# An output stage's quarters, casts and finishing steps spread out, V's casts moved, and two attention slivers joined

## The chip, the cores and the metric

The kernel runs on one core of a Trainium2 chip. The time is device microseconds from launch to end; before the change the median of three runs is 2045.68 us (2044.66 to 2046.22). The core has an engine for matrix products (PE), a vector engine (DVE), a scalar engine (ACT), a small general one (POOL) and a queue that issues the transfers (SP). Each works through its own instructions in order, and a semaphore holds an instruction back until what it reads is there.

## The reference

One inference step of a hybrid decoder layer: 1024 prompt tokens with 16 learned ones ahead of them, and 8 × 4 sample tokens. The input is normalised and multiplied by one large projection. Half of the width goes to eight heads of stick-breaking attention, half to gated linear attention; both are gated and go through one output projection, then a norm and the residual.

```python
def stick_break_weights(z, mask):
    sp = jnp.where(mask, jax.nn.softplus(z), 0.0)
    later = lax.cumsum(sp, axis=z.ndim - 1, reverse=True) - sp
    return jnp.where(mask, jnp.exp(jax.nn.log_sigmoid(z) - later), 0.0)

def sb_attend(qb, qpos, k, v, kpos, bias):
    a = stick_break_weights(sb_logits(qb, k, bias), kpos[None, :] < qpos[:, None])
    return jnp.einsum('bhqk,bkhd->bqhd', a.astype(v.dtype), v)
...
    mixed = jnp.concatenate([o_sb * jax.nn.silu(sg), o_gla * jax.nn.silu(gg)], axis=-1)
    return mixed @ w_out
```

The sum `later` runs over the keys behind a key, so a block of keys needs the sum of all later blocks first. The result y is x plus the norm of `mixed @ w_out`.

## The kernel before

Every product is made of three matmuls: both operands are split into a high part (a cast to a shorter float, on ACT) and a low part (the difference, on DVE), and hi·hi, hi·lo and lo·hi are added up in PSUM, the memory of 8 banks that PE writes. So each weight tile that arrives (`wr`) costs an ACT cast and a DVE subtraction before PE can use it.

**The order of work.** The stages of the program run one after another: norm and transposes; eight heads; low rank and gates; gated linear attention; the paged values of the samples, with the gate groups; the output stage. Inside a stage a small scheduler of generators, the Weaver `W`, interleaves side work with the products: after a group of products `W.beat()` runs the generators that are due, and `yield n` in a generator means "go on n beats later". A generator only writes instructions down; a list scheduler then orders them on each engine. `spread(ins)` ties an instruction behind the latest marked product `W.mark`, and the manual dependencies called "behind" tie it behind another instruction. Both tie only the order in which the scheduler places instructions; neither makes an engine wait.

**The heads** (L541 to L760). While the input projection of head h runs, the attention of head h−1 is woven in. `attend_tile` makes one tile: keys of block j (126 new keys each) against queries of half qi. It makes z (L609 to L611), a softplus X on ACT (L615 to L619) and DVE (L620), masks on POOL (L623, L639), takes the carry of the block behind (L629), splits X (`hi_s`, `lo_s`, L590 and L593), adds the sums with a triangular matrix (L632, L633), makes Y by an exponential (L637), splits it (`hi_a`, `lo_a`) and multiplies by V into the bank O (L647 to L649). The tiles of a half go from the last block to the first; the half qi = 1 begins with (1,8), 32 queries wide, and qi = 0 with (0,4), 24 wide. The other tiles have 150 to 512 queries. `load_v` (L570 to L585) loads three pieces of V (`vr`), casts them (L582) and takes the low part (L584).

**The output stage** (L1325 to L1690). The projection is made by seven products p of halves of the matrices, in Strassen's manner: pairs (1,2), (6), (5,3) and (7,4), each for q = 0 and 1. A step (p, q) has eight k, and each k takes a weight tile (`ring`, cast at L1429, low part at L1430) and twelve matmuls of 128x512 (L1631 to L1633), four banks by three. `W.beat()` follows each k. Left operands are the forms `f`: quarters of the mixed matrix, loaded from `md` by `quarter` (L1333), added or subtracted (`s3` at L1343, `s2` at L1348, `combined`), and cast (L1375, L1378). `take` empties banks at the end of a step (`u` copies at L1478, sums at L1496 and L1500). `finish0` (L1540 to L1577) finishes the first half of the rows: it loads x (`xr`, L1554), forms y = y · r + x on DVE (L1565) and stores it; afterwards it loads the residual of the second half (L1557). `load_keep` loads and casts eight weight tiles for the last step, and `finish_samples` finishes the sample rows. Each DMA of the queue waits for the eighth before it, and the rings of raw tiles (four of tag `fr`, seven of tag `wr`) are passed on in order.

Of the kernel before, what the change touches and what calls it, by code (L numbers as in the profile page):

```python
# [20 lines left out]
P = 128  # L21
# [19 lines left out]
KT = 126  # L41
# [48 lines left out]
def hybrid_step(ctx: ExitStack, tc: tile.TileContext, x_prompt, x_sample, cache_k, cache_v, state_gla,  # L90
# [447 lines left out]
    with tc.tile_pool(name="sp", bufs=1) as sp, tc.tile_pool(name="sps", bufs=1, space=PSUM) as sps:  # L538
# [5 lines left out]
        cap = sp.tile([P, 1], F32, name="cap")  # L544
        pool.memset(cap[:], 16.0)
        room = sp.tile([P, HEADS], F32, name="room")
        vec.tensor_scalar(room[:], bias0[:], -1.0, 16.0, ALU.mult, ALU.add)
# [22 lines left out]
        def load_v(h, V, behind):  # L570

            for c in range(3):
# [6 lines left out]
                if c == 2:  # L579
                    nc.sync.dma_start(sv[1:33, 2, :], src[8 * KT:REAL])  # L580
                vs = slice(3 * c, 3 * c + 3)
                ins = act.copy(V[0][:, vs, :], sv)  # L582
                tc.add_manual_dep(ins.ins, behind.name, NOSYNC, reason="behind")
                vec.tensor_tensor(V[1][:, vs, :], sv, V[0][:, vs, :].bitcast(F32), ALU.subtract)  # L584
# [13 lines left out]
        def attend_tile(h, qi, qlo, qhi, j, jmax, q, kt, V, carry, O):  # L598
            nm = f"{h}_{qi}_{j}"
            k0 = j * KT  # L600
            nk = P
            c0 = max(qlo, k0)
            col = c0 - qlo
            n = qhi - c0
            qs = slice(c0 - META, c0 - META + n)
            ks = slice(j * P, j * P + nk)
            z = sps.tile([P, 512], F32, tag="z", bufs=4, name=f"z{nm}")
            zz = z[:nk, :n]
            mm(zz, kt[0][:, ks], q[0][:, qs], start=True, stop=False)  # L609
            mm(zz, kt[0][:, ks], q[1][:, qs], start=False, stop=False)  # L610
            mm(zz, kt[1][:, ks], q[0][:, qs], start=False, stop=True)  # L611
# [6 lines left out]
            act.activation(X, X, AF.Exp, scale=-1.0, bias=cap[:nk])  # L618
# [3 lines left out]
            if w > 0:  # L622
                pool.affine_select(X[:, :w], X[:, :w], [[1, w]], ALU.is_gt, 0.0, base=c0 - k0 + 1, channel_multiplier=-1)  # L623
            yield 2
            if j < jmax:
# [8 lines left out]
            carry[qi] = (j, zz, col)  # L634
# [3 lines left out]
            if w > 0:  # L638
                pool.affine_select(Y[:, :w], Y[:, :w], [[1, w]], ALU.is_gt, 0.0, base=c0 - k0 + 1, channel_multiplier=-1)  # L639
# [10 lines left out]
            if j == 0:  # L650
                st = sp.tile([P, 512], F32, tag="X", bufs=3, name=f"ost{h}_{qi}")
                act.copy(st[:], o[:])
                nc.sync.dma_start(od[h][:, qlo - META:qhi - META], st[:])

        def attend(h, q, kt, V):

            carry, O = {}, {}
            for qi, j in ORDER:
                qlo, qhi = ((16, 528), (528, REAL))[qi]
                n = qhi - max(qlo, j * KT)  # L660
                W.spawn(attend_tile(h, qi, qlo, qhi, j, (qhi - 1) // KT, q, kt, V, carry, O))
# [3 lines left out]
        ORDER = [(1, j) for j in range(8, -1, -1)] + [(0, j) for j in range(4, -1, -1)]  # L665
# [6 lines left out]
        def sample_q(h, qsm, ks):  # L672
# [8 lines left out]
            zns = sp.tile([NSMP, NSMP], F32, tag="zns", name=f"zns{h}")  # L681
            act.copy(zns[:], ps[:NSMP, :NSMP])
            nc.sync.dma_start(znd[:, h, :], zns[:])
# [3 lines left out]
        def head(h):  # L687
# [21 lines left out]
            def split_k(raw, c, lo, hi):  # L709
# [10 lines left out]
                if c == 2:  # L720
                    act.copy(ks[:], raw[:, REAL - lo:hi - lo])
# [603 lines left out]
    with ExitStack() as out:  # L1325
# [26 lines left out]
        for k in range(6):  # L1352
            W.spawn(later(k), 26 + 2 * k)
# [29 lines left out]
        def combined(p, k):  # L1383
# [3 lines left out]
            t = quarter(raw(f"q{p}_{k}")[:], p == 4, p in (2, 3, 4), k)  # L1387
# [5 lines left out]

        def form(p, gap):
            if p == 3:
# [334 lines left out]
```

## Time and profile before

| what | value |
|---|---|
| median of the runs | 2045.68 us (2044.66 to 2046.22) |
| the profiled execution, its own time | 2047.26 us |
| its span, first to last instruction | 2045.6 us |
| mean granted PE clock | 0.998 |
| DVE line L470 (scores against paged keys) | 595.0 us, 2048 of 291 ns |
| longest wait of PE, at start-up (L233) | 8.1 us |
| DMA over the span | 301.85 MB, 148 GB/s |

A timeline row gives start, duration, engine, line, operation, written tile <- read tiles, and shape; "x2" joins neighbours of one kind. In square brackets stands how long the engine was idle ahead of it, and which instruction or DMA released it. Where a row says `[0.92 <-DVE lo_s L593]`, PE did nothing for 0.92 us until DVE had written `lo_s`. Matmuls overlap, so the price of one is read from the distance of starts, not from durations. Queries by window give each engine's busy time, the granted clock, the share of the 16 DMA engines and GB/s.

### The profile page before, as it was taken

The numbers are of one execution on the slowest core, as the hardware profiler recorded it, in microseconds if no ns is written. First come the engines' busy times: TensorE is split into PE (matmuls) and PEld (weight loads), VectorE is DVE, ScalarE is ACT, GpSimd is POOL, SyncE is SP. The second block draws the span as 40 slices with busy tenths as digits, with TensorE's granted clock in tenths as the row PEclk, the third lists the DMA queues.
The fourth block names the chain that finished last, engine by engine and source line by source line (L and its number), as shares of the span: only waits on it lengthen the run. The fifth ranks groups of instructions, "written<-read, shape, count | busy, mean of one in ns | idle before, by whom it ended". The sixth has DMA issues, their size and how long they took to land.

```text
span 2045.6 us, 41995 instructions
## 1 busy us (share of the span) xinstructions
PE 2012.9 (98%) x12443; PEld 1859.9 (91%) x12443; DVE 1499.0 (73%) x6171; ACT 1025.6 (50%) x2409; POOL 93.9 (5%) x339
## 2 busy tenths in 40 slices
PE   6999999999999999999999999999999999999998
PEld 5999999999999999999999999999988898788776
DVE  7368888888888888899898888978444347554576
ACT  7366767675766758433535345254334335432332
POOL 0011110101000000100000000000000000000000
PEclk9999999999999999999999999999999999999999
DMA  6355454544555442533343424336767666352475
GB/s 203 101 142 159 131 163 135 163 136 152 154 154 145 144 128 77 141 103 88 104 107 81 130 78 121 89 90 189 237 217 237 223 216 191 130 169 76 145 257 196
DMA packets 371822, 301.85 MB, mean 148 GB/s; under 512 B 42360, under 2 KB 312104, under 8 KB 371592
## 3 DMA queue, kind: packets, MB, share of 16 engines
q1 hardware_dynamic: 371288, 298.64, 48.7%
q8 instruction: 98, 1.61, 0.3%
q14 instruction: 132, 1.08, 0.2%
q10 hardware_dynamic: 304, 0.53, 0.1%
HBM read 241.75 MB, written 57.31 MB: 146 GB/s over the span
## 4 chain that ended last, share of the span: by engine, by line
PE 89%; DMA 4%; DVE 4%; ACT 2%; issue 1%; SPq 1%; DVEq 0%; ACTq 0%
PE acc_g L347 5%; PE acc_g L348 5%; PE acc_g L349 5%; PE b L1631 4%; PE b L1633 4%; PE b L1632 4%; PE acc_gv L347 3%; PE acc_gv L348 3%; PE acc_gv L349 3%; PE acc_k L347 3%; PE acc_k L349 3%; PE acc_k L348 3%; PE acc_q L347 3%; PE acc_q L348 3%; PE acc_q L349 3%; PE acc_v L347 3%
## 5 line engine op out<-in xcount | busy, mean ns | idle before, releaser
L470 DVE SCALAR_TENSOR_TENSOR jk<-kp,qb 128x128 f32<-128x128 f32 x2048 | 595.0, 291 | 44.8 <-DMA qb<-qsd 1.7
L347 PE MATMUL acc_g<-hT,wh_g 128*128 128x368 f32 (+2 forms) x768 | 251.0, 327 | 1.0 <-ACT gx L532 1.0
L348 PE MATMUL acc_g<-hT,wh_g 128*128 128x368 f32 (+2 forms) x768 | 247.2, 322 | 0.0
L349 PE MATMUL acc_g<-hT,wl_g 128*128 128x368 f32 (+2 forms) x768 | 246.9, 322 | 0.0
L470 DVE DVE_READ_ACCUMULATOR jk<-kp,qb 128x1 f32 x2048 | 169.4, 83 | 0.0
L1631 PE MATMUL b<-ring,f 128*128 128x512 f32 x416 | 164.8, 396 | 2.5 <-DVE u L1500 1.1
L1632 PE MATMUL b<-ring,f 128*128 128x512 f32 x416 | 163.2, 392 | 1.0 <-DVE ring L1430 1.0
L1633 PE MATMUL b<-ring,f 128*128 128x512 f32 x416 | 162.5, 391 | 0.0
L347 PEld LDWEIGHTS acc_g<-hT,wh_g 128*128 128x128 f32 x768 | 144.3, 188 | 13.3 <-issue 10.7
L1430 DVE TENSOR_TENSOR ring<-wr,ring 128x512 fp32r<-128x512 f32 x104 | 71.2, 690 | 106.0 <-ACT ring L1429 103.9
L348 PEld LDWEIGHTS acc_g<-hT,wh_g 128*128 128x128 f32 x768 | 144.5, 188 | 0.7
L349 PEld LDWEIGHTS acc_g<-hT,wl_g 128*128 128x128 f32 x768 | 144.2, 188 | 0.0
L1429 ACT CAST ring<-wr 128x512 fp32r<-128x512 f32 x104 | 64.2, 621 | 144.4 <-PE b L1633 89.9
L347 PE MATMUL acc_gv<-hT,wh_gv 128*128 128x402 f32 (+2 forms) x384 | 130.1, 339 | 0.0
L347 PE MATMUL acc_k<-hT,wh_k 128*128 128x384 f32 (+1 forms) x384 | 126.1, 328 | 0.0
L348 PE MATMUL acc_gv<-hT,wh_gv 128*128 128x402 f32 (+2 forms) x384 | 125.3, 326 | 0.0
L349 PE MATMUL acc_gv<-hT,wl_gv 128*128 128x402 f32 (+2 forms) x384 | 125.0, 326 | 0.0
L347 PE MATMUL acc_q<-hT,wh_q 128*128 128x368 f32 (+2 forms) x384 | 125.0, 325 | 0.0
L349 PE MATMUL acc_k<-hT,wl_k 128*128 128x384 f32 (+1 forms) x384 | 124.7, 325 | 0.0
L348 PE MATMUL acc_k<-hT,wh_k 128*128 128x384 f32 (+1 forms) x384 | 124.6, 325 | 0.0
L348 PE MATMUL acc_q<-hT,wh_q 128*128 128x368 f32 (+2 forms) x384 | 123.6, 322 | 0.0
L349 PE MATMUL acc_q<-hT,wl_q 128*128 128x368 f32 (+2 forms) x384 | 123.3, 321 | 0.0
(468 smaller groups left out, 5292.7 us busy)
## 6 DMA issues: line engine op xcount, KB each, us to landing
kp<-in_cache_k_dram SPq DMA_DIRECT2D x512, 64.0 KB, 2.0
vr<-in_cache_v_dram SPq DMA_DIRECT2D x64, 512.0 KB, 5.1
qb<-qsd SPq DMA_DIRECT2D x64, 256.0 KB, 5.6
wr_g<-in_w_in_dram SPq DMA_DIRECT2D x64, 256.0 KB, 3.5
wr<-td SPq DMA_DIRECT2D x56, 256.0 KB, 2.8
tf<-in_w_out_dram SPq DMA_DIRECT2D x48, 256.0 KB, 4.9
td<-tf SPq DMA_DIRECT2D x48, 256.0 KB, 2.5
wr<-in_w_out_dram SPq DMA_DIRECT2D x48, 256.0 KB, 3.5
```

What stands on the lines that cost most here:

```text
L347: mm(acc[c][:, :n], wh, hh[k][:, lo:hi], start=(k == 0), stop=False)
L348: mm(acc[c][:, :n], wh, hl[k][:, lo:hi], start=False, stop=False)
L349: W.mark = mm(acc[c][:, :n], wl, hh[k][:, lo:hi], start=False, stop=(k == NK - 1)).ins
L470: ins = vec.scalar_tensor_tensor(jk[:], kp[:], 1.0, qbs[h, b][:, t, :], ALU.mult, ALU.mult, accum_out=zt[:, t, NPG - 1 - i:NPG - i])
L1429: act.copy(wh, r)
L1430: vec.tensor_tensor(wl, r, wh.bitcast(F32), ALU.subtract)
L1631: mm(bk[:], ah, wh, start=first and k == 0, stop=False, skip_group_check=True)
L1632: mm(bk[:], ah, wl, start=False, stop=False, skip_group_check=True)
L1633: mm(bk[:], al, wh, start=False, stop=last and k == 7, skip_group_check=True)
```

## The change

The diff has three parts.

**One tile for two slivers.** The tiles (1,8) and (0,4) become one tile (`both`) with 64 queries: columns 480 to 511 of both halves of q. Its keys are block 8's, with the 24 keys of block 4 that (0,4) used copied by POOL to rows 32 to 55 of the block; V's rows get the same by a small load, and the masks on POOL cut off what is not to be seen. The carry of half 0 is copied by ACT (`kept`), the product goes to the O bank, is copied by ACT (`ob`), and each half of it is added to the last 32 columns of that half's output on DVE.

```diff
-        def attend_tile(h, qi, qlo, qhi, j, jmax, q, kt, V, carry, O):
+        def attend_tile(h, qi, qlo, qhi, j, q, kt, V, carry, O):
...
-            n = qhi - c0
+            n = 64 if both else qhi - c0
...
+            def queries(t):
+                if both:
+                    return t[:].rearrange("p (a x) -> p a x", a=2)[:, :, 480:512]
+                return t[:, qs]
+
+            def causal(t):
+                if both:
+                    t = t.rearrange("p (a x) -> p a x", a=2)
+                    pool.affine_select(t, t, [[1 - 24, 2], [1, 32]], ALU.is_gt, 0.0, base=24, channel_multiplier=-1)
+                    pool.memset(t[0:32, 0, :], 0.0)
...
+            if both:
+                kept = sp.tile([P, NSMP], F32, tag="ks", name=f"cy{h}")
+                act.copy(kept[0:1, :], z[0:1, 0:32])
+                carry[0], carry[1] = (4, kept, 480), (8, z[:, 32:64], 480)
+            else:
+                carry[qi] = (j, zz, col)
...
+            if both:
+                o = sps.tile([P, 512], F32, tag="O", name=f"Ob{h}")[:, :n]
+                mm(o, V[0][:, j, :], ah[:, :n], start=True, stop=False, skip_group_check=True)
+                mm(o, V[0][:, j, :], al[:, :n], start=False, stop=False, skip_group_check=True)
+                mm(o, V[1][:, j, :], ah[:, :n], start=False, stop=True, skip_group_check=True)
+                O[2] = sp.tile([P, 64], F32, tag="ob", name=f"ob{h}")
+                act.copy(O[2][:], o)
+                return
...
+                vec.tensor_tensor(st[:, 480:512], st[:, 480:512], O[2][:, 32 * qi:32 * qi + 32], ALU.add)
...
-        ORDER = [(1, j) for j in range(8, -1, -1)] + [(0, j) for j in range(4, -1, -1)]
+        ORDER = [(1, j) for j in range(8, -1, -1)] + [(0, j) for j in range(3, -1, -1)]
...
+                    for t in kt:
+                        pool.tensor_copy(t[:, 8 * P + 32:8 * P + 56], t[:, 4 * P + 1:4 * P + 25].bitcast(F32))
```

On PE, in head 0's attention beside the products for k of head 1 (`acc_k1`), before had the three z matmuls of the tile (0,4), of 24 columns (`z0_0_4` is z of head 0, half 0, block 4):

```order
L348 MATMUL acc_k1_0_1897<-hT11_156,wh_k1_2_2202 128x384
L349 MATMUL acc_k1_0_1897<-hT11_156,wl_k1_2_2203 128x384
L609 MATMUL z0_0_4_2277<-q0_0_1077,k0_0_846 128x24
L610 MATMUL z0_0_4_2277<-q1_0_1078,k0_0_846 128x24
L611 MATMUL z0_0_4_2277<-q0_0_1077,k1_0_847 128x24
L347 MATMUL acc_k1_1_1898<-hT10_155,wh_k1_2_2202 128x384
L348 MATMUL acc_k1_1_1898<-hT10_155,wh_k1_2_2202 128x384
```

At the same rows after has the z of the tile (0,3), 150 columns wide:

```order
L348 MATMUL acc_k1_0_1905<-hT11_156,wh_k1_2_2210 128x384
L349 MATMUL acc_k1_0_1905<-hT11_156,wl_k1_2_2211 128x384
L630 MATMUL z0_0_3_2285<-q0_0_1077,k0_0_844 128x150
L631 MATMUL z0_0_3_2285<-q1_0_1078,k0_0_844 128x150
L632 MATMUL z0_0_3_2285<-q0_0_1077,k1_0_845 128x150
L347 MATMUL acc_k1_1_1906<-hT10_155,wh_k1_2_2210 128x384
L348 MATMUL acc_k1_1_1906<-hT10_155,wh_k1_2_2210 128x384
```

The three rows of 24 columns are gone, and (0,3) has moved up into their place; the joined tile stands where (1,8) stood, beside the products for v of head 1, with 64 columns instead of 32:

```order
L349 MATMUL acc_v1_1_1307<-hT1_146,wl_v1_0_1312 128x384
L630 MATMUL z0_1_8_1339<-q0_0_1077,k0_0_844 128x64
L631 MATMUL z0_1_8_1339<-q1_0_1078,k0_0_844 128x64
L632 MATMUL z0_1_8_1339<-q0_0_1077,k1_0_845 128x64
L347 MATMUL acc_v1_2_1308<-hT0_145,wh_v1_0_1311 128x304
```

What moved: 24-column rows are gone, and the half 0 starts with (0,3). In all PE has 11262 rows before and 11198 after.

**V's casts.** `load_v` issues all three loads first, the last piece ahead, and casts them some beats later, each tied to a product.

```diff
-            for c in range(3):
+            rows = []
+            for c in (2, 1, 0):
...
+                rows.append((vs, sv))
+                yield 1
+            yield 1
+            for vs, sv in rows:
                 ins = act.copy(V[0][:, vs, :], sv)
                 tc.add_manual_dep(ins.ins, behind.name, NOSYNC, reason="behind")
+                spread(ins)
```

On ACT, in head 4, the last V cast of before (L582) stands ahead of the whole X chain of the tile (1,7) (`X4_1_7`, L615 to L619):

```order
L682 COPY zns4_8416<-zn4_8414 32x32
L582 CAST V0_4_8310<-vr4_2_8397 128x384
L615 ACTIVATE X4_1_7_8427<-z4_1_7_8423,room_837 128x158
L618 ACTIVATE X4_1_7_8427<-X4_1_7_8427,cap_835 128x158
L619 ACTIVATE X4_1_7_8427<-X4_1_7_8427 128x158
L187 CAST wh_v5_2_8617<-wr_v5_2_8615 128x512
L637 ACTIVATE Y4_1_8_8478<-z4_1_8_8362,bias0_827 128x32
L629 ACTIVATE X4_1_7_8427<-z4_1_8_8362 1x32
L590 CAST hi_s4_1_7_8502<-X4_1_7_8427 128x158
```

In after two casts (L587) stand among that chain and the third behind it:

```order
L636 ACTIVATE X4_1_7_8367<-z4_1_7_8363,gpre_78 128x158
L639 ACTIVATE X4_1_7_8367<-X4_1_7_8367,gpre_78 128x158
L587 CAST V0_4_8254<-vr4_2_8271 128x384
L640 ACTIVATE X4_1_7_8367<-X4_1_7_8367 128x158
L587 CAST V0_4_8254<-vr4_1_8301 128x384
L187 CAST wh_v5_2_8566<-wr_v5_2_8564 128x512
L587 CAST V0_4_8254<-vr4_0_8340 128x384
L657 COPY cy4_8422<-z4_1_8_8304 1x32
L663 ACTIVATE Y4_1_8_8424<-z4_1_8_8304,bias0_827 128x64
L650 ACTIVATE X4_1_7_8367<-z4_1_8_8304 1x32
L596 CAST hi_s4_1_7_8449<-X4_1_7_8367 128x158
```

The X operations now come first; behind the third cast are the carry copy `cy4`, the Y of the joined tile and the carry and `hi_s` of (1,7).

**The output stage.** `early` loads a11 and s3 16 beats apart, `later` starts four beats later, `form` fetches its quarters two ahead and pins the casts of p = 2 from k = 4 on behind the newest `u` copy; quarter loads are tied to products, whose last matmul is now `W.mark` (so `spread` works in this stage). `finish0` takes 1 or 2 beats by turns, ties its DVE operation to a product, and loads the second half's first residuals between its items; `finish_samples` begins three beats later.

```diff
         def quarter(dst, r, c, k):
-            nc.sync.dma_start(dst, md[8 * c + k][:, 512 * r:512 * r + 512])
+            spread(nc.sync.dma_start(dst, md[8 * c + k][:, 512 * r:512 * r + 512]))
...
             quarter(a11[k], 0, 0, k)
+            yield 16
             quarter(s3[k], 1, 0, k)
-            yield 5
+            yield 9
...
-            W.spawn(later(k), 26 + 2 * k)
+            W.spawn(later(k), 30 + 2 * k)
...
-            t = quarter(raw(f"q{p}_{k}")[:], p == 4, p in (2, 3, 4), k)
+            t = quarters.pop((p, k))
...
+            def fetch(k):
+                if k < 8 and p not in (1, 6, 7):
+                    quarters[p, k] = quarter(raw(f"q{p}_{k}")[:], p == 4, p in (2, 3, 4), k)
+
+            if p not in (1, 6, 7):
+                fetch(0)
+                fetch(1)
+                yield 2
...
+                    fetch(k + 2)
+                    while p == 2 and k == 4 and not newest_u:
+                        yield 1
+                    split(f[:, 0], f[:, 1], combined(p, k), (newest_u if k > 3 else evacs)[-1] if p == 2 else None)
...
-                yield 2 if n < 8 else 1
+                yield 2 - n % 2
                 o = sums_[i, b]
-                vec.scalar_tensor_tensor(o, o, r[:, i:i + 1], xs.pop(n), ALU.mult, ALU.add)
+                spread(vec.scalar_tensor_tensor(o, o, r[:, i:i + 1], xs.pop(n), ALU.mult, ALU.add))
...
+                elif n > 7:
+                    i, b = divmod(n - 8, 2)
+                    xr[i, b] = late_[b][:, i * 512:(i + 1) * 512].bitcast(F32)
+                    load_xr(i, b)
...
         def finish_samples():
-            yield 2
+            yield 5
...
-            mm(bk[:], al, wh, start=False, stop=last and k == 7, skip_group_check=True)
+            W.mark = mm(bk[:], al, wh, start=False, stop=last and k == 7, skip_group_check=True).ins
```

On DVE, at the end of step (4,0) and the start of step (7,1), before has ring splits (L1430; `wr71_0` is the weight tile of p = 7, q = 1, k = 0), casts' low parts of `keep` (L1673), the finishing operations of `finish0` (L1565, with `xr1_2` the x of row block 1, column block 2) and the sums `u0` that empty the banks (L1500):

```order
L1673 TENSOR_TENSOR keep3_30995<-keep3_30995 128x512
L1430 TENSOR_TENSOR ring1_29199<-wr40_7_31304,ring0_29198 128x512
L1565 SCALAR_TENSOR_TENSOR y12_0_1_30594<-y12_0_1_30594,vrt_y0_30976,xr1_2_31299 128x512
L1673 TENSOR_TENSOR keep3_30995<-keep3_30995 128x512
L1430 TENSOR_TENSOR ring1_29199<-wr71_3_31408,ring0_29198 128x512
L1565 SCALAR_TENSOR_TENSOR y12_1_1_30937<-y12_1_1_30937,vrt_y0_30976,xr1_3_31362 128x512
L1430 TENSOR_TENSOR ring1_29199<-wr71_0_31342,ring0_29198 128x512
L1565 SCALAR_TENSOR_TENSOR y12_0_2_30599<-y12_0_2_30599,vrt_y0_30976,xr2_2_31384 128x512
L1565 SCALAR_TENSOR_TENSOR y12_1_2_30942<-y12_1_2_30942,vrt_y0_30976,xr2_3_31406 128x512
L1500 TENSOR_TENSOR u0_0_29405<-b70_0_30952,u0_0_29405 128x512
L1500 TENSOR_TENSOR u0_1_29407<-b70_1_30953,u0_1_29407 128x512
L1500 TENSOR_TENSOR u0_2_29409<-b70_2_30954,u0_2_29409 128x512
```

In after the same stretch reads (ring splits at L1481, finishing at L1616, sums at L1551, `keep` at L1724):

```order
L1724 TENSOR_TENSOR keep3_30879<-keep3_30879 128x512
L1616 SCALAR_TENSOR_TENSOR c11_0_29119<-c11_0_29119,vrt_y0_30857,xr3_0_30983 128x512
L1481 TENSOR_TENSOR ring1_29084<-wr40_7_31201,ring0_29083 128x512
L1616 SCALAR_TENSOR_TENSOR c11_1_29120<-c11_1_29120,vrt_y0_30857,xr3_1_31004 128x512
L1481 TENSOR_TENSOR ring1_29084<-wr71_3_31306,ring0_29083 128x512
L1724 TENSOR_TENSOR keep3_30879<-keep3_30879 128x512
L1481 TENSOR_TENSOR ring1_29084<-wr71_0_31244,ring0_29083 128x512
L1616 SCALAR_TENSOR_TENSOR y12_0_0_30475<-y12_0_0_30475,vrt_y0_30857,xr0_2_31075 128x512
L1481 TENSOR_TENSOR ring1_29084<-wr71_1_31262,ring0_29083 128x512
L1551 TENSOR_TENSOR u0_0_29289<-b70_0_30833,u0_0_29289 128x512
L1551 TENSOR_TENSOR u0_1_29291<-b70_1_30834,u0_1_29291 128x512
L1551 TENSOR_TENSOR u0_2_29293<-b70_2_30835,u0_2_29293 128x512
```

Before has three finishing operations between the split of `wr71_3` and the sums `u0_0`, two of them next to each other; after has one there, and those ahead of it belong to the first two column blocks (`c11`), each with a ring split or a `keep` part behind it.

More of the change, by code (lines that the diff above doesn't have):

```diff
@@ L543, in hybrid_step @@
         pool.affine_select(bias0[:], bias0[:], [[0, HEADS]], ALU.is_gt, -1e30, base=P - 1, channel_multiplier=-1)
[L544 to L547, printed above, removed]
+        cap, room = gpre[:, 0:1], gpre[:, HEADS:]
+        pool.memset(cap, 16.0)
+        vec.tensor_scalar(room, bias0[:], -1.0, 16.0, ALU.mult, ALU.add)
         def tok_out(raw, c, lo, hi, h, outp, outs_, nm):
@@ L637, in attend_tile @@
             act.activation(Y, zz, AF.Exp, bias=bias)
[L638 to L639 removed]
+            causal(Y)
             if w > 0:
@@ L680, in sample_q @@
             mm(ps[:NSMP, :NSMP], ks[:], qsm[:], start=True, stop=True)
-            zns = sp.tile([NSMP, NSMP], F32, tag="zns", name=f"zns{h}")
-            act.copy(zns[:], ps[:NSMP, :NSMP])
-            nc.sync.dma_start(znd[:, h, :], zns[:])
+            zns = stage(f"zns{h}")[:NSMP, :NSMP]
+            act.copy(zns, ps[:NSMP, :NSMP])
+            nc.sync.dma_start(znd[:, h, :], zns)
             yield 4
@@ L1439, in hybrid_step @@
             W.spawn(later(k))
-        W.spawn(form(2, 1), 2)
+        W.spawn(form(2, 1), 1)
         W.spawn(form(6, 2), 10)
@@ L1477, in take @@
                 with urgent():
-                    act.copy(u, bk[:])
+                    newest_u.append(act.copy(u, bk[:]).ins)
             elif p == 2:
```

38 lines of the change are left out of this document (19 added, 19 removed).

## The prediction

> **What bounds the kernel now.** The page comes first.
>
> ```profile
> span 2045.6 us, 41995 instructions
> ...
> PE 2012.9 (98%) x12443; PEld 1859.9 (91%) x12443; DVE 1499.0 (73%) x6171; ACT 1025.6 (50%) x2409; POOL 93.9 (5%) x339
> ...
> PE 89%; DMA 4%; DVE 4%; ACT 2%; issue 1%; SPq 1%; DVEq 0%; ACTq 0%
> ```
>
> PE, the matmul engine, is busy for 98% of the span and is 89% of the chain that ended last. So only two things shorten the kernel: fewer PE instructions, or a wait of PE that goes. The windows by stage show where PE stands.
>
> ```profile
> 105.00:830.00 725.00, 723.82 (x4458) 698.10 (x4457) 596.60 (x2822) 490.95 (x1122) 72.40 (x236) 1.00 0.49 142
> ...
> 1680.00:1900.00 220.00, 217.53 (x1104) 176.00 (x1103) 125.39 (x209) 93.56 (x182) 0.15 (x1) 1.00 0.46 149
> 1900.00:2000.00 100.00, 97.89 (x465) 77.22 (x463) 61.19 (x103) 35.79 (x75) 0.00 (x0) 0.98 0.58 195
> ```
>
> After the window the first figure is its length, the second PE's busy time; the third from the end is the granted clock. The heads (105 to 830) leave 1.2 us without PE work, so there a gain comes from instructions. From 1680 to 2000 PE lacks 4.6 us, and the clock falls below 1 once. The list of PE's waits names their releasers (total, times, longest).
>
> ```profile
> PE z L633 <- DVE lo_s L593: 1.2, 2, 0.9
> PE b L1631 <- DVE u L1500: 1.1, 1, 1.1
> PE acc_g L347 <- ACT gx L532: 1.0, 1, 1.0
> ```
>
> **Term 1, the slivers.** Each head had a tile of 32 columns and one of 24, eight matmuls each (three z, two triangular, three O). They become one tile of 64 columns, so eight matmuls a head go, 64 in all. The timeline of PE shows the price of one.
>
> ```profile
> 116.13 0.18 PE L609 MATMUL z<-q,k 128*128 128x32 f32 x1
> 116.16 0.26 PE L610 MATMUL z<-q,k 128*128 128x32 f32 x1
> 116.27 0.26 PE L611 MATMUL z<-q,k 128*128 128x32 f32 x1
> 116.38 0.38 PE L347 MATMUL acc_v<-hT,wh_v 128*128 128x304 f32 x1
> 116.60 0.30 PE L348 MATMUL acc_v<-hT,wh_v 128*128 128x304 f32 x1
> 116.74 0.30 PE L349 MATMUL acc_v<-hT,wl_v 128*128 128x304 f32 x1
> ...
> 118.88 0.28 PE L610 MATMUL z<-q,k 128*128 128x158 f32 x1
> 119.00 0.28 PE L611 MATMUL z<-q,k 128*128 128x158 f32 x1
> 119.11 0.38 PE L347 MATMUL acc_v<-hT,wh_v 128*128 128x384 f32 x1
> ```
>
> From the first z to the second product stand 116.60 − 116.13 = 0.47 us. Products alone start 0.14 apart (116.60 to 116.74), so three slivers cost 0.33, or 0.11 each. I take the 24-column matmuls, which have no rows here, at the same 0.11. Matmuls of 158 columns also start 0.11 to 0.12 apart: in this range the columns don't set the pace, and the 64-column tile costs what the 32-column one did. If its 32 more columns counted at the rate of 512 columns in 0.227 us (1984.71 to 1984.93 below), they would add 0.014 × 64 = 0.9 us; the bounds are 0 and 0.9, and I take 0, by the 158-column rows. Gain: 64 × 0.11 = **7.0 us**, bounds 6.1 and 7.0.
>
> The Trainium skill, "TensorE: Matmul & The Clock Gate", section "Back-to-back issue gap", gives matmuls of 1 to 64 columns about 25 ns apart; by it the term would be an estimated 1.6 us. The trace doesn't agree: each matmul here has its own 128-column weights, and starts lie 110 ns apart.
>
> What the joined tile adds lies on other engines: per head two copies on ACT, two additions on DVE, two casts of 24 columns and a memset on POOL (5% busy) and one small DMA, against a whole tile's chain that goes. The POOL casts stand some 150 PE rows ahead of their first reader. Two additions touch PE: the carry for (0,3) comes from a copy, which is done many tiles earlier, and the joined product takes the one O bank until ACT has copied it, with 24 PE rows before the next tile's O. I take both at 0; the price without that cover is the third rival's.
>
> **Term 2, the V casts.** One wait of the heads is theirs.
>
> ```profile
> 489.90 0.51 ACT L582 CAST V<-vr 128x384 fp32r<-128x384 f32 x1 [3.38 <-DMA vr<-out_dram]
> 490.32 0.39 ACT L615 ACTIVATE X<-z,room 128x158 f32<-128x158 f32 x1
> ...
> 494.27 0.34 PE L633 MATMUL z<-lo_s,ntri 128*128 128x158 f32 x1 [0.92 <-DVE lo_s L593]
> ...
> 485.16 0.37 SPq L580 DMA_DIRECT2D vr<-out_dram x1
> ```
>
> In head 4 ACT stands 3.38 us at a cast whose load was issued at 485.16 and used at 489.90, 4.7 us later; the tile's X is behind it, and at the end PE waits 0.92. In the order of after, that tile's X operations stand ahead of two of the three casts. But the last load has its cast only 20 PE rows behind it, about 3.3 us at 0.17 each, where 4.7 are needed, and the carry and hi_s of the same tile are queued behind that cast. So about 1.4 us of ACT's wait stays, partly covered. Bounds 0 and 0.9; I take **0.6**. In the other heads the load lies 30 to 100 rows ahead.
>
> **Term 3, the output stage.** Four places.
>
> ```profile
> 1680.41 0.32 PE L349 MATMUL acc_g<-hT,wl_g 128*128 128x368 f32 x1
> 1681.79 0.45 PE L347 MATMUL acc_g<-hT,wh_g 128*128 128x384 f32 x1 [1.05 <-ACT gx L532]
> ...
> 1679.23 0.69 DVE L1343 TENSOR_TENSOR s<-s,a 128x512 f32<-128x512 f32 x1 [0.65 <-DMA s<-md]
> ...
> 1680.86 0.51 ACT L517 ACTIVATE gs<-gs 128x368 f32<-128x368 f32 x1 [2.47 <-DVE gs L516]
> ```
>
> First: 1681.79 − 1680.41 − 0.17 = 1.2 us. DVE stood at a subtraction of quarters whose load came late, ACT behind DVE's gs, and PE behind ACT's gx. In after, only one such subtraction stands ahead, 36 PE rows (6 us) behind its loads.
>
> ```profile
> 1723.91 0.39 PE L1633 MATMUL b<-ring,f 128*128 128x512 f32 x1
> ...
> 1725.82 0.40 PE L1631 MATMUL b<-ring,f 128*128 128x512 f32 x1
> ...
> 1730.04 0.50 PE L1631 MATMUL b<-ring,f 128*128 128x512 f32 x1 [0.98 <-ACT u L1478]
> ...
> 1723.15 0.62 ACT L1375 CAST f<-q 128x512 fp32r<-128x512 f32 x1 [3.44 <-DMA q<-md]
> ...
> 1727.33 0.62 ACT L1375 CAST f<-q 128x512 fp32r<-128x512 f32 x1 [2.17 <-DMA q<-md]
> ```
>
> Second and third: ACT waits 3.44 and 2.17 us for quarters, with ring casts and the u copies queued behind. Four starts from 1723.91 to 1725.82 take 1.91 instead of 4 × 0.227, which loses 1.0; the other place loses 0.98. In after the loads run two quarters ahead, and the casts from k = 4 on stand behind the u copies.
>
> ```profile
> 1984.71 0.39 PE L1633 MATMUL b<-ring,f 128*128 128x512 f32 x1
> 1984.93 0.39 PE L1631 MATMUL b<-ring,f 128*128 128x512 f32 x1
> 1986.13 0.50 PE L1632 MATMUL b<-ring,f 128*128 128x512 f32 x1 [0.81 <-DVE ring L1430]
> ...
> 1988.69 0.80 PE L1631 MATMUL b<-ring,f 128*128 128x512 f32 x1 [1.13 <-DVE u L1500]
> ...
> 1992.45 0.39 PE L1631 MATMUL b<-ring,f 128*128 128x512 f32 x1
> ...
> 1984.72 0.75 DVE L1565 SCALAR_TENSOR_TENSOR y<-y,vrt_y,xr 128x512 f32<-128x512 f32 x1 [2.48 <-DMA xr<-in_x_prompt_dram]
> ...
> 1984.00:1988.00 4.00, 2.75 (x11) 1.61 (x9) 2.74 (x5) 0.00 (x0) 0.00 (x0) 1.00 1.06 407
> 1988.00:1992.00 4.00, 3.31 (x8) 2.66 (x9) 4.00 (x8) 3.33 (x10) 0.00 (x0) 0.59 0.56 216
> ```
>
> Fourth, the largest: 15 starts from 1984.93 to 1992.45 take 7.52 us instead of 15 × 0.227 = 3.4, so 4.1 go. DVE stands at finishing operations of L1565 for xr, with the ring split and the u sums that PE wants behind them; then the clock falls to 0.59 on average. In before's order the load stands 12 or 13 products ahead (some 2.9 us). In after it stands 53 to 71 ahead, at least 12 us.
>
> The Trainium skill, same page, section "HAM oscillation — how this bites in real kernels", says that an idle window of about 3.4 us brings the clock down. Here waits of 0.81 and 1.13 us with matmuls between them sufficed, so the trace differs. By the page two new waits of 1 us would cost 2 us; by these rows they can cost nearly twice that.
>
> Together 1.2 + 1.0 + 1.0 + 4.1 = **7.3 us** if nothing takes their place. Something may: the order now brings eight residual loads of 256 KB forward, into a stretch where the DMA engines were full (1.06, 407 GB/s), and the "keep" loads have casts ahead of ring casts, with a margin of 0 to 1 us. In the second place a subtraction of a late quarter still stands ahead of one ring split. I bound new and left waits by 0 and 4.1 (one more such place as the fourth) and take **0.8**, the size of its shorter wait, 0.81. The tail after the last product (some 9 us) keeps its work; it is taken at 0 change.
>
> **Sum.** 7.0 + 0.6 + 7.3 − 0.8 = 14.1 us. The profiled execution took 2047.26 us in all, its span and 1.66 around it, so it would become 2033.2. The median of the runs, 2045.68, is 1.6 lower; from it, **2031.6**.
>
> **Rivals.** (a) The output stage's waits re-form: what DVE and ACT no longer wait for at one place they wait for at the next, since the bytes stay the same. Then terms 1 and 2 remain: 2045.68 − 7.6 = 2038.1. For it speaks the DMA share of 1.06; against it that xr's lead grows from 2.9 to 12 us or more. (b) Slivers cost only their columns, as the page has it: 24 columns at 0.227 us for 512 are 0.011 us, 64 of them 0.7, and the time would be 2045.68 − (0.7 + 0.6 + 7.3 − 0.8) = 2037.9. The 0.11 spacing speaks against it. (c) Slower: in every head PE waits at the O bank, because ACT's copy of the joined product is late. All else as forecast, the kernel is level at 14.1 / 8 = 1.8 us a head, and slower by over 0.2% (4.1 us, about what a measurement can tell) from 18.2 / 8 = 2.3; a wait as ACT's 3.38 at V, met in full in each head, would give 2031.6 + 27.0 = 2058.6. For it: ACT is strictly in order, and such a wait is seen. Against it: that wait of 3.38 reached PE as 0.92, and in one head of eight.
>
> **Chances.** The forecast with its bounds 0.63; (a) 0.27, of which 0.06 end within 0.2%; (b) 0.02; (c) 0.05, of which 0.04 are slower and 0.01 within; 0.03 for several small losses that end within. So faster 0.86, within 0.10, slower 0.04. The range goes from 2029.2 (terms at their upper bounds, 7.0 + 0.9 + 7.3 = 15.2, no new wait, 0.3 of shorter waits, and the 1.0 by which the fastest run, 2044.66, lies below the median) to 2038.7, where term 1 alone is left.
>
> **What would show it.** Right: 64 fewer matmuls and the heads some 7 us shorter; no PE wait over 0.5 us at the four places; the clock at 1.00 from 1900 to 2000 of before. Wrong: a sliver tile that costs more than 0.33 us for its z; an ACT copy of O in PE's list of waits; DVE waits for xr or for keep in front of a ring split; a second fall of the clock.

## The result and the profile after

The kernel takes 2034.3 us (median of 6 runs, 2033.18 to 2034.95) against 2045.88 us (6 runs, 2043.53 to 2046.51): a ratio of 0.9942, interval 0.9932 to 0.9952, or 11.6 us less between the medians. The forecast was 2031.6 with 2029.2 to 2038.7. The profiled execution took 2034.71 us, 12.55 less than that of before.

The page of the changed kernel, in the rows that were shown of before:

```profile
span 2033.0 us, 41746 instructions
...
PE 2004.2 (99%) x12379; PEld 1852.4 (91%) x12379; DVE 1496.9 (74%) x6163; ACT 1018.4 (50%) x2377; POOL 96.1 (5%) x355
...
PE 91%; DVE 3%; DMA 2%; ACT 2%; issue 1%; SPq 0%; DVEq 0%; POOL 0%; POOLq 0%; ACTq 0%
```

PE has 64 instructions fewer and 8.7 us less busy time; DVE has nearly all of its work still (2.1 us less). The windows by stage of the same execution:

```profile
105.00:830.00 725.00, 724.54 (x4439) 698.41 (x4438) 601.65 (x2842) 486.75 (x1098) 73.58 (x252) 1.00 0.50 142
...
1680.00:1900.00 220.00, 220.00 (x1106) 177.78 (x1105) 124.05 (x204) 88.49 (x168) 0.26 (x1) 1.00 0.46 151
1900.00:2000.00 100.00, 98.53 (x489) 77.42 (x491) 60.41 (x103) 36.37 (x79) 0.00 (x0) 1.00 0.66 221
```

From 1680 to 1900 PE no longer waits, and the clock stays at 1.00. From 1900 to 2000 1.47 us are still lost. The list of PE's waits says where (start-up left out):

```profile
PE b L1682 <- DVE y L1547: 1.1, 1, 1.1
PE acc_gk L347 <- ACT gx L532: 1.0, 1, 1.0
...
PE b L1682 <- DVE u L1551: 0.3, 1, 0.3
...
PE z L654 <- DVE lo_s L599: 0.3, 1, 0.3
```

Only the wait at acc_gk has no counterpart in before. The one at y stood at the same place there with 0.17 us and has grown; the one at u is what is left of the fourth place, where it was 1.13; and the one at z is in before too, at 0.27, as the smaller of the two in its list. Where the 12.55 us came from is read off the starts of the same PE rows in the two timelines:

| PE row | before | after | gained since the row above |
|---|---|---|---|
| first acc_ga (end of the heads' projections) | 757.88 | 750.94 | 6.94 |
| first acc_gk | 862.09 | 854.64 | 0.51 |
| first acc_gq | 886.17 | 879.95 | −1.23 |
| acc_g of group 3 | 1339.05 | 1333.12 | −0.29 |
| first matmul of step (1,0) | 1703.79 | 1695.98 | 1.88 |
| step (2,0) | 1730.04 | 1720.15 | 2.08 |
| step (4,0) | 1963.06 | 1954.15 | −0.98 |
| step (7,1) | 1984.93 | 1976.03 | −0.01 |
| step (4,1) | 2013.21 | 2000.82 | 3.49 |
| end of the span | 2045.56 | 2033.00 | 0.17 |

### The profile page after: what moved, and what is told of

Read it like the earlier page. It is cut to its first block, busy times and chain, and to the rows that moved or that the text cites. A ratio compares the mean times of both kernels' runs of the same rounds, so it can differ in the third digit from the quotient of the medians.

```text
span 2033.0 us, 41746 instructions
## 1 busy us (share of the span) xinstructions
PE 2004.2 (99%) x12379; PEld 1852.4 (91%) x12379; DVE 1496.9 (74%) x6163; ACT 1018.4 (50%) x2377; POOL 96.1 (5%) x355
## 4 chain that ended last, share of the span: by engine, by line
PE 91%; DVE 3%; DMA 2%; ACT 2%; issue 1%; SPq 0%; DVEq 0%; POOL 0%; POOLq 0%; ACTq 0%
PE acc_g L347 6%; PE acc_g L348 5%; PE acc_g L349 5%; PE b L1682 4%; PE b L1683 4%; PE b L1684 4%; PE acc_gv L347 3%; PE acc_gv L348 3%; PE acc_gv L349 3%; PE acc_k L347 3%; PE acc_k L349 3%; PE acc_k L348 3%; PE acc_q L348 3%; PE acc_q L347 3%; PE acc_q L349 3%; PE acc_v L347 3%
## 5 line engine op out<-in xcount | busy, mean ns | idle before, releaser
L1481 DVE TENSOR_TENSOR ring<-wr,ring 128x512 fp32r<-128x512 f32 x104 | 71.2, 689 | 97.7 <-ACT ring L1480 97.1
```

What stands on the lines that cost most here:

```text
L1481: vec.tensor_tensor(wl, r, wh.bitcast(F32), ALU.subtract)
```

## The experiments

Times are medians; a figure "against before" is the ratio with its interval, taken with the runs of the kernel before on the same chip. Those runs spread from 2043.6 to 2050.7 us, so an interval is some 2 us wide to each side, and small terms are read from the traces.

**1. The sliver tile alone** (e1_slivers). The hunks on `attend_tile`, `ORDER`, k's copied columns and the small load of V, put into before:

```diff
-        ORDER = [(1, j) for j in range(8, -1, -1)] + [(0, j) for j in range(4, -1, -1)]
+        ORDER = [(1, j) for j in range(8, -1, -1)] + [(0, j) for j in range(3, -1, -1)]
```

> The joined sliver tile alone, put into the kernel before; V's casts and the output stage are as before. Theory (each small matmul costs 0.11 us, the pace of its weight load): 64 fewer matmuls, 7.0 us less. If DVE's backlog of score operations at the end of the heads comes from PE being faster there, the new wait of about 1.1 us at the gate groups (ACT gx behind DVE gs) shows here too, and the gain is about 5.9. Rival (a small matmul costs only its columns): 0.7 us less. The wait of 0.9 us at V in head 4 and the four places of the output stage stay.

Measured: 2040.91 us, 0.998 against before (0.997 to 0.9989), so 2 to 6 us less and not 7. Its nine runs spread from 2039.01 to 2045.53, and the profiled one, 2039.07, is among the fastest. In its trace a part of the 7 us comes back as waits. One is at the gate groups (1.3 us at acc_gk, as expected); the other, in head 5, was not expected. Timeline of PE and of ACT there:

```profile
573.95 0.41 PE L347 MATMUL acc_v<-hT,wh_v 128*128 128x304 f32 x1 [0.96 <-ACT qsm L772]
...
573.28 0.51 ACT L582 CAST V<-vr 128x384 fp32r<-128x384 f32 x1 [1.00 <-DMA vr<-out_dram]
```

ACT stands at a cast of V, and the copy `qsm` that frees PE's bank is behind it. So in this execution the old place of V's casts cost another wait. Runs 10 and 11, which have the old casts too, show a smaller one of the same kind (0.3 and 0.2 us at `qsm`); none of the eight profiles with the later casts has it. That the later casts keep it off is read from these traces; no run adds them to the slivers alone.

**2. The output stage alone** (e2_output): all hunks from `quarter` on, in before.

```diff
-            W.spawn(later(k), 26 + 2 * k)
+            W.spawn(later(k), 30 + 2 * k)
...
-                yield 2 if n < 8 else 1
+                yield 2 - n % 2
```

> The output stage's part alone, put into the kernel before. Theory: the four waits go (7.3 us) and two new ones come, behind the keep casts, together about 1.8 us: 5.5 us less. Rival (the waits only move, since DMA is full): no more than 2 us less, with a fall of the clock in the records as before.

Measured: 2041.2 us, 0.9976 (0.9967 to 0.9985), 3 to 7 us less. Its profiled execution took 2041.09, 6.2 below the profile of before. PE's wait at y, which was expected, is not in this trace; the one at u is (0.3). The rival, no more than 2 us, falls.

**3. V's casts alone** (e3_vcasts): the hunk of `load_v` without the small load, in before.

```diff
-            for c in range(3):
+            for c in (2, 1, 0):
...
+                spread(ins)
```

> V's loads first and casts later, alone, put into the kernel before. Theory: the wait of 0.92 us in head 4 goes, 1.0 us less. Rival (the late load has its cast only some 20 products behind it): 0.4 us or less, with a wait of about 0.5 us left at the same place.

Measured: 2045.88 us, 1.0 (0.9991 to 1.0009). The wait in head 4 isn't in its trace, but 0 to 1.8 us either way is all that the time can say. Run 6 explains why it is so little: the wait isn't in every execution of before. Of the five profiles whose heads are those of before, the first has it at 0.92 us and run 2 at 0.38; runs 6, 10 and 11 don't have it. By the medians of runs 1 to 3, each against before on the same chip, the three parts alone give 5.2, 4.9 and 0.2 us, 10.3 together, of 11.6 for the whole change.

This trace also shows that the wait at y needs no change of the output stage: with the stage of before, 1.20 us stand at y (1962.35), behind finishing operations at which DVE waited 1.2 and 0.5 us for loads of x.

**4. Keep casts tied to products** (e4_keep_tied), in the changed kernel:

```diff
-                    act.copy(wh, wl.bitcast(F32))
-                    vec.tensor_tensor(wl, wl.bitcast(F32), wh.bitcast(F32), ALU.subtract)
+                    spread(act.copy(wh, wl.bitcast(F32)))
+                    spread(vec.tensor_tensor(wl, wl.bitcast(F32), wh.bitcast(F32), ALU.subtract))
```

> The changed kernel, with the cast and the low part of each keep tile tied to a product eight beats behind its load. Theory (the keep loads come late and DVE and ACT stand at them, ahead of the sums that empty the banks): the waits of 1.13 us at y and 0.34 us at u go, and the time falls by 1.5 to 1.8 us against the changed kernel. Rival (the waits come from the finishing operations or from DVE's own load in that stretch): no change beyond 0.3 us, and waits at the same two places.

The wait at y in the changed kernel, in its timelines of ACT, DVE and PE:

```profile
1950.79 1.28 ACT L1723 CAST keep<-keep 128x512 fp32r<-128x512 f32 x2 [2.74 <-DMA keep<-td]
...
1951.44 0.69 DVE L1724 TENSOR_TENSOR keep<-keep 128x512 fp32r<-128x512 f32 x1 [2.36 <-ACT keep L1723]
...
1953.31 1.88 DVE L1547 TENSOR_TENSOR y<-b,y 128x512 f32<-128x512 f32 x3
...
1954.15 0.47 PE L1682 MATMUL b<-ring,f 128*128 128x512 f32 x1 [1.13 <-DVE y L1547]
```

ACT waits for a keep load, DVE for ACT, and the sums y that empty PE's banks stand behind both. With the casts tied, the same places read:

```profile
1950.51 2.48 DVE L1547 TENSOR_TENSOR y<-b,y 128x512 f32<-128x512 f32 x4
...
1952.85 0.50 PE L1682 MATMUL b<-ring,f 128*128 128x512 f32 x1
```

Both waits are gone, and the profiled execution, which is level with that of the changed kernel to 0.1 us at 1940, ends 2.0 us earlier (spans of 2031.0 and 2033.0). The median is 2033.71, 0.994 against before (0.9927 to 0.9954), 0.6 below the changed kernel's 2034.3; the intervals don't separate the two. The waits at y and u are absent in runs 8 and 9 too, which have the same ties. Without the ties the wait at y is 1.13 us in the changed kernel and 1.63 (run 7), 1.14 (run 5) and 0.40 (run 12) in the others, and the stage alone (run 2) has none. So the cause is shown, its price by the two traces is about 1.9 us, and the medians leave open how much of that a usual run has.

**5. The gate operation on POOL** (e5_gs_on_pool), groups 0 to 2, in the changed kernel:

```diff
-        vec.tensor_scalar(s, x, -1.0, 30.0, ALU.mult, ALU.min)
+        (pool if g < 3 else vec).tensor_scalar(s, x, -1.0, 30.0, ALU.mult, ALU.min)
```

> The changed kernel, with the first operation of the gate (gs = min(-x, 30), L516) of the gate groups 0 to 2 on POOL instead of DVE. Theory (DVE's in-order queue of score operations runs behind PE at the end of the heads, and ACT and PE wait for the gate operation in it): the wait of 0.96 us at acc_gk goes, about 1.1 us less than the changed kernel in an execution that has the wait. Rival (ACT or PE is late for another reason): the wait stays or is as long.

The wait that is meant: in before DVE made gs at 860.93 and PE came to acc_gk at 862.09, so gs was 1.2 us early. In the changed kernel (timelines of DVE, ACT and PE) PE came at 854.64:

```profile
855.54 0.34 DVE L516 TENSOR_SCALAR gs<-gx 128x368 f32<-128x368 f32 x1
...
855.91 0.51 ACT L517 ACTIVATE gs<-gs 128x368 f32<-128x368 f32 x1 [2.48 <-DVE gs L516]
...
856.84 0.44 PE L347 MATMUL acc_gk<-hT,wh_gk 128*128 128x386 f32 x1 [0.96 <-ACT gx L532]
```

Now gs is 0.9 us late: DVE has lost 2.1 us against PE (run 7 shows where). On POOL the wait shrinks to 0.2 us:

```profile
PE acc_gk L347 <- ACT gx L532: 0.2, 1, 0.2
```

but the time is 2035.71 us (0.9941, 0.9928 to 0.9955), against 2034.55 for the changed kernel on the same chip (run 7): the 1.1 us less that was expected didn't come. DVE, in the same window (750 to 870), now waits at the gates' later steps, which in the changed kernel aren't among its eight longest waits there:

```profile
DVE gs L519 <- ACT gs L518: 3.1, 3, 2.1
DVE gs L521 <- ACT gs L520: 1.8, 2, 0.9
```

PE starts acc_gk at 856.12 instead of 854.64: 0.80 of that lies ahead of the first acc_ga (751.74 against 750.94) and 0.68 behind it. The 0.80 is not the edit's: it is a wait of 0.90 us in head 0, at 130.63, such as the second profile of before (0.91) and run 4 (0.82) have too. Behind it two waits of 0.28 and 0.21 us stand at the last attention tile, near 810, which only this run and run 8 have. So PE did wait for DVE's gs, since with gs off DVE the wait shrinks; why gs was late on DVE this run doesn't say. What is gained at acc_gk is lost around it.

**6 and 7. The two kernels a second time** (e6_before_again, e7_after_again), unchanged.

> The kernel before, unchanged, profiled a second time. Theory (the profile that the sum was made against had waits that a usual execution has only in part; it took 1.4 us more than the median): the gate wait at 1680, the sum of the output stage's waits or the clock's fall differ by 1 us or more between the two profiles. Rival (the waits are fixed by the order): the same waits within 0.2 us each, and the same total within 0.5 us.

> The changed kernel, unchanged, profiled a second time, on the same chip as the others of this call. Theory: the waits at y and u behind the keep casts are there again (1 to 1.8 us), the wait at acc_gk may be there or not; the time is 2034 within 1.5. Rival (they were accidents of one execution): no wait over 0.3 us at y and u.

Before: 2046.15 us, its second profile 2047.42. In head 4 PE's row of the V wait (timeline of the second profile):

```profile
494.63 0.23 PE L632 MATMUL z<-hi_s,ntri 128*128 128x158 f32 x1
494.78 0.34 PE L633 MATMUL z<-lo_s,ntri 128*128 128x158 f32 x1
```

There is no wait. Instead one of 0.91 us stands in head 0, at 131.10, and the wait at acc_g near 1680 is 0.6 instead of 1.05. Near 1985, in the same timeline, and the window there:

```profile
1985.09 0.39 PE L1631 MATMUL b<-ring,f 128*128 128x512 f32 x1
1987.08 0.50 PE L1632 MATMUL b<-ring,f 128*128 128x512 f32 x1 [1.61 <-DVE ring L1430]
...
1989.67 0.50 PE L1631 MATMUL b<-ring,f 128*128 128x512 f32 x1 [1.16 <-DVE u L1500]
...
1992.06 0.50 PE L1632 MATMUL b<-ring,f 128*128 128x512 f32 x1 [0.50 <-DVE ring L1430]
...
1992.63 0.39 PE L1631 MATMUL b<-ring,f 128*128 128x512 f32 x1
...
1988.00:1992.00 4.00, 2.40 (x10) 1.31 (x8) 3.74 (x7) 2.35 (x7) 0.00 (x0) 1.00 0.81 310
```

The waits are longer than in the first profile and the clock doesn't fall; the 15 starts from 1985.09 to 1992.63 take 7.54 us, where the first profile, with the fall, had 7.52. So the loss is the same 4.1 us, but made otherwise. In the second profile DVE's sums u begin 3.8 us after the first of these starts, and in the first 3.0 us, because xr comes later. In the first profile the ring part of the 13th matmul was ready at 1991.04 and PE, slowed, came to it at 1991.84; from these rows I estimate 0.7 us for the fall, and 3.4 of the 4.1 for DVE. Between 1720 and 1992 the places of the output stage are the same in both profiles; their sizes, the wait at 1680 and the small waits of the heads are not.

After: 2034.55 us, second profile 2033.78. The wait at y is there again (1.6), that at u too (0.3); that at acc_gk isn't. Between the second profiles of the two kernels lie 13.64 us (2047.42 and 2033.78), against 12.55 between the first. What DVE waited for between 800 and 858, in the first profile of the changed kernel:

```profile
DVE wal L862 <- ACT wal L861: 1.7, 1, 1.7
DVE gs L522 <- DMA go<-od: 1.1, 1, 1.1
```

and in the second:

```profile
DVE gs L522 <- DMA go<-od: 1.0, 1, 1.0
...
DVE wal L862 <- ACT wal L861: 0.4, 1, 0.4
```

The operation at wal is the first that DVE has for the next stage (the low part of a small weight, after ACT's cast of it). In ACT's and DVE's timelines it and gs stand so, in the first profile of the changed kernel (its gs is the row at 855.54 in run 5):

```profile
841.91 0.30 ACT L861 CAST wal<-walr 96x128 fp32r<-96x128 f32 x1 [3.75 <-DMA od<-ost]
...
842.34 0.28 DVE L862 TENSOR_TENSOR wal<-walr,wal 32x128 fp32r<-32x128 f32 x1 [1.67 <-ACT wal L861]
```

in the second:

```profile
840.56 0.30 ACT L861 CAST wal<-walr 96x128 fp32r<-96x128 f32 x1 [2.42 <-DMA od<-ost]
...
840.99 0.28 DVE L862 TENSOR_TENSOR wal<-walr,wal 32x128 fp32r<-32x128 f32 x1 [0.43 <-ACT wal L861]
...
854.19 0.35 DVE L516 TENSOR_SCALAR gs<-gx 128x368 f32<-128x368 f32 x1
```

and in before:

```profile
848.73 0.28 DVE L826 TENSOR_TENSOR wal<-walr,wal 32x128 fp32r<-32x128 f32 x1 [1.23 <-ACT wal L825]
...
860.93 0.35 DVE L516 TENSOR_SCALAR gs<-gx 128x368 f32<-128x368 f32 x1
```

From wal to gs DVE takes 13.2 us in both profiles of the changed kernel and 12.2 in before: 36 scores lie between them instead of 33, as in every run that has the joined tile and gs on DVE. So the new order takes 1.0 us of the 1.2 by which gs was early. Whether PE waits is then decided at wal. In the second profile wal comes early enough that gs, at 854.19, is 0.4 us ahead of PE's 854.63; in the first it comes 1.35 us later, because ACT stands at its cast until 841.91, by its row for a store (`od<-ost`). The wait for go, which before doesn't have in this stretch, lies ahead of wal, where DVE has to wait in any case. And no backlog is carried over from the heads: at 829.86, ahead of all this, DVE stood 0.79 us waiting for ACT's gx.

**8. Both** (e8_keep_and_gs): the edits of 4 and 5 together.

> The changed kernel with both: keep casts tied to products and the gate operation of groups 0 to 2 on POOL. If both waits were real and independent: 2.5 to 3 us below the changed kernel in the profile, and 1 to 2.5 by the medians. If one of them only moved: no better than the better of the two alone.

2033.53 us, 0.9935 (0.9922 to 0.9949); profile 2033.26. It is like keep alone (2033.71, 2032.66), so the POOL part adds nothing, as in 5.

**9. Keep, and the gate's last product later** (e9_keep_and_go):

```diff
+        if g == 0:
+            yield 8
+            spread(vec.tensor_tensor(s[:, :w], s[:, :w], o[:, :w], ALU.mult))
```

> The changed kernel with keep casts tied to products and, in gate group 0, the last product of the gate (it waits for the load of go, whose data the last attention tile stores) eight beats later. Theory (DVE falls behind PE at the end of the heads in part because it stands 1.0 to 1.5 us at that product): DVE's wait for go goes, the gate operation of group 2 starts about 1 us earlier against acc_gk, no wait at acc_gk; against the kernel with keep alone 0 to 1 us less. Rival (DVE's lag comes from its score operations alone): the same start against acc_gk within 0.3 us.

2034.0 us, 0.9933 (0.9919 to 0.9947). The edit missed: it moves the last product of group 0 (its third piece starts at 815.47 instead of 808.59), but the wait for go between 800 and 858 is that of group 1. DVE's waits in that stretch, and PE's, are

```profile
DVE wal L866 <- ACT wal L865: 1.4, 1, 1.4
DVE gs L526 <- DMA go<-od: 1.2, 1, 1.2
...
PE acc_gk L347 <- ACT gx L536: 0.9, 1, 0.9
```

The wait for go stayed (1.1 in the changed kernel), so this run doesn't test it. It agrees with the reading of run 7: the wait at wal is a long one, and the wait at acc_gk is there again. Of the six profiles with the joined tile and gs on DVE, three have the wait at acc_gk (0.9 to 1.3 us); in them ACT stood 3.6 to 4.2 us ahead of the cast of wal (the first profile, runs 1 and 9). In the three without it, ACT stood 2.4 to 2.5 us (runs 4, 7 and 12). No run moves that store, so that it decides is read from rows and not shown.

**10 and 11. The two halves of the output stage** in before: the finishing part with the mark in the products (e10_finish), and the quarters and casts (e11_quarters).

> Of the output stage only the finishing part (items by turns of 1 and 2 beats, tied to products; the second half's residual loads between them; the mark in the products), in the kernel before. Theory: the waits at ring and u near 1985 and the clock's fall go (4.1 us), the three waits between 1680 and 1730 stay, and the keep casts may cost up to 2: 2 to 4 us less. Rival (they go only together with the quarters): under 1 us.

> Of the output stage only the quarters and casts (early, later, fetching two ahead, casts behind u), in the kernel before. Theory: the waits at 1680, 1724 and 1729 go (2.5 to 3.2 us), those near 1985 with the clock's fall stay: 2.5 to 3.2 us less. Rival (the waits re-form): under 1 us.

Finishing: 2043.6 us, 0.9984 (0.9974 to 0.9993); one of its 11 runs took 7029 us, which the median passes over. Its list of PE's waits from 1660 on:

```profile
PE b L1631 <- ACT u L1478: 1.0, 1, 1.0
PE b L1631 <- ACT ring L1429: 0.9, 1, 0.9
PE b L1631 <- DVE u L1500: 0.4, 1, 0.4
```

The waits near 1985 are down to 0.4 at u, those between 1720 and 1730 have stayed. The one at acc_g near 1680 is down to 0.3, though the quarters are those of before; runs 1 and 3 don't have it at all, so it too comes and goes. Quarters: 2043.02 us, 0.9982 (0.9973 to 0.9991). Its windows:

```profile
1680.00:1900.00 220.00, 220.00 (x1120) 179.07 (x1119) 130.23 (x217) 93.72 (x182) 0.26 (x1) 1.00 0.50 160
1900.00:2000.00 100.00, 97.50 (x479) 76.19 (x479) 59.95 (x100) 35.22 (x75) 0.00 (x0) 1.00 0.59 195
```

Here the first stretch is free of waits. In the second the waits near 1985 are still there (0.9 and 0.5 at ring, 1.1 at u), but the clock stays at 1.00. So in the traces each half takes its own places. By the medians they give 3.0 us and 3.6 us, and together 4.9 (run 2); with intervals of 2 us to each side that they add up is not shown.

**12. Twelve more small matmuls a head** (e12_sliver_x5), in the changed kernel; the three z matmuls of the joined tile are repeated, and only the last ones count:

```diff
+            for _ in range(5 if both else 1):
-            mm(zz, kt[0][:, ks], queries(q[0]), start=True, stop=False)
+                mm(zz, kt[0][:, ks], queries(q[0]), start=True, stop=False)
```

> The changed kernel with the three z matmuls of the joined tile made five times over in each head (each time from the start, so only the last counts): 96 matmuls of 64 columns more. Theory (each costs 0.11 us, the pace of its weight load): 10.6 us more. Rivals: by the columns (64 of 512 at 0.227) 2.7 us more; by the Trainium skill's figure of about 25 ns, 2.4 us more.

Its timeline of PE in head 0, and the first row of acc_gk:

```profile
116.46 0.28 PE L632 MATMUL z<-q,k 128*128 128x64 f32 x1
116.57 0.28 PE L633 MATMUL z<-q,k 128*128 128x64 f32 x1
116.69 0.28 PE L631 MATMUL z<-q,k 128*128 128x64 f32 x1
...
117.80 0.28 PE L632 MATMUL z<-q,k 128*128 128x64 f32 x1
...
865.39 0.34 PE L347 MATMUL acc_gk<-hT,wh_gk 128*128 128x402 f32 x1
```

From the start at 116.46 to that at 117.80 it is twelve matmuls and 1.34 us, 0.112 each, at 64 columns. Up to acc_gk the 96 matmuls cost 865.39 − 854.64 = 10.75 us, which is 96 × 0.112: both rivals (2.4 and 2.7) fall. The whole time is 2043.59 us, only 9.3 more than the changed kernel's 2034.3: in its trace the wait at acc_gk isn't there and the wait at y is 0.4. The first is not the slower PE's doing. DVE's gs starts at 865.03, 0.36 us ahead of acc_gk, as in run 7 (0.44), whose PE is 10.8 us faster; and PE is slower here than in before, where gs was 1.2 ahead. So it is not that DVE falls behind a faster PE.

## Why the prediction was right, and what was mis-sized

**What bounds the kernel.** Right: PE is at 99% after, and both sources, fewer instructions and waits that go, gave their part.

**Term 1, 7.0 us.** The price of 0.11 us and its independence of the columns hold (run 12). From the first product for v of one head to that of the next, where neither kernel waits, before takes 91.70 us (297.52 to 389.22) and after 90.82 (296.08 to 386.90): 0.88 a head, 7.0 in eight. That ACT and POOL work added to it costs nothing held too: no wait of PE names the copy of O. What had no term is the margin of the other engines' operations: gs on DVE was 1.2 us early, and the new order puts three more scores ahead of it. So a late wal gave the wait at acc_gk, 1.2 us of starts in one profile and none in the other (run 7).

**Term 2, 0.6 us.** The size was that of one execution: the second profile of before hasn't the wait. Three of the six profiles with the old casts have a wait in head 4 (0.92, 0.49 and 0.38 us; first, runs 1 and 2), none of the eight with the later ones. On its own the edit gives nothing measurable.

**Term 3, 7.3 us.** By starts the four places and a wait in the linear attention that I had not counted gave 7.4 us in the first pair of profiles (1.2 and 0.65, 2.1, 3.5) and 7.1 in the second (1.4, 2.1, 3.5). Runs 10 and 11 take the halves of the stage apart. The second, third and fourth place go for the reasons given. The first is down or absent without the quarters too (runs 10, 1 and 3), so its 1.2 us were in part those of one execution. The fourth gave 3.5 instead of 4.1, since a wait of 0.3 stays at u. That its loss was nearly twice its waits was laid to the fall of the clock; by the rows of run 6 the fall made some 0.7 us of it, and without it PE would have met a third wait for DVE.

**New waits, 0.8 us.** This is the term that was mis-sized. By starts 2.2 us were lost at new or grown waits in the first pair (1.23 at acc_gk and 0.98 at y) and 1.6 in the second (y alone). The keep loads, named as a risk with a margin of 0 to 1 us, cost PE 1.1 and 1.6 us at y in the two profiles. Run 4 shows the keep part; the wait at acc_gk was in no term.

**The base.** The sum was made from an execution that lay 1.4 us above the median and was then taken off the median. Profile against profile 14.1 us were forecast and 12.55 and 13.64 came; median against median 11.6. Both profiled executions of before lie 1.3 to 1.4 above the median of their runs, those of the changed kernel 0.4 above and 0.8 below. Of the 2.7 us by which the forecast misses the median, 1.5 are by the first pair the new waits, and the other 1.2 come from this base. Which waits an execution of the median time lacks is not known, since none was profiled.

**Rivals.** (a), all of the output stage's waits re-form, falls: of the 7.4 and 7.1 us by starts, 6.5 and 5.5 stay gained after the loss at y. (b) falls by run 12. (c), a wait at the O bank, is in no trace.

Three versions stand slightly below the changed kernel: keep casts tied to products (2033.71), that with the gate on POOL (2033.53), and run 9 (2034.0). No interval separates them from it.

## What to carry to other kernels

When an order is changed, look how early each operation is that the bounding engine will wait for: here gs was 1.2 us early, three more operations ahead of it took 1.0 of that, and with so little left a store that came late in some executions became a wait. Ties that only order instructions don't know when a load lands: a cast of a late load must be placed by products behind it, or everything else on that engine waits with it. And take a second profile of the kernel before the sum is made: waits of 1 us come and go between executions of the same program, and only those that stand in both are worth counting in full.

## What the runs showed of the hardware

The fall of the clock does not follow from the size of the waits. In the first profile of before, waits of 0.81 and 1.13 us near 1985 were followed by a mean clock of 0.59 from 1988 to 1992; in the second, waits of 1.61 and 1.16 us at the same place left the clock at 1.00. Runs 1, 3 and 11 have waits of 0.9 to 1.2 us there too, and the clock stays at 1.00, so it fell in one of five profiles. The Trainium skill, "TensorE: Matmul & The Clock Gate", section "What's actually happening", calls the window that is watched free-running; that would make such a fall a matter of where the window lies, and these profiles agree with it, though the position of the window isn't recorded.
